# Feed-forward in a two-block transformer kernel: sixteen of 22 inner chunks as Strassen products of halves

## The chip, the core and the metric

One core of a Trainium2 chip runs the whole program. The metric is device time in microseconds (us) of one execution; lower is better. Three runs of the kernel before took 3705.26, 3708.18 and 3711.72 us, median 3708.18.

## The reference, cut to what matters

The program is two blocks of a network on 512 tokens of width 1024. The change touches only the feed-forward of the second block, which runs four times (`ffn1` and `ffn2` in each of two layers):

```python
D_MODEL, SEQ, DEPTH = 1024, 512, 2
D_FF = ((8 * D_MODEL // 3 + 127) // 128) * 128      # 2816 = 22 chunks of 128
def rmsnorm(x, g):
    xf = x.astype(jnp.float32)
    y = xf * lax.rsqrt(jnp.mean(xf * xf, axis=-1, keepdims=True) + NORM_EPS)
    return (y * g.astype(jnp.float32)).astype(x.dtype)
def swiglu(h, w_in, w_out):
    gate, up = jnp.split(h @ w_in, 2, axis=-1)
    return (jax.nn.silu(gate) * up) @ w_out
# per layer:
x = x + 0.5 * swiglu(rmsnorm(x, ffn1_norm[layer]), ffn1_w_in[layer], ffn1_w_out[layer])
...
x = x + 0.5 * swiglu(rmsnorm(x, ffn2_norm[layer]), ffn2_w_in[layer], ffn2_w_out[layer])
```

All of it is float32.

## The kernel before

Activations lie feature-major: `self.x` is eight tiles of 128 features by 512 tokens. A float32 product is made of three TensorE products in the format float32r: `split` (lines 112 to 115) writes a high part (a rounded copy, on ScalarE, L114) and a low part (the difference, on VectorE, L115), and `mm3` (L131 to L133) adds high·high, low·high and high·low in PSUM. `weight` loads 128x1024 weights (512 KB) by the SP queue (L121) into one of three staging buffers, and splits them into `wh` and `wl` (four buffers each). `fm` does one such load and its matmuls: for a chunk of 128 output features, 8 blocks of 128 inputs, so 8 x 3 = 24 matmuls with 128x128 stationary weights and 512 moving columns (the tokens).

`ffn` (L1185) goes over the 22 inner chunks in three groups of 8, 8 and 6. A chunk takes two `fm`, one for the gate and one for the up part, 48 matmuls. The normalisation's factor per token, `rb`, is not in the moving tiles: it is multiplied in afterwards, on VectorE into the gate (L1196), after the SiLU (L1197, ScalarE) once more on GpSimd (L1198); then VectorE multiplies by the up part (L1200) and the result is split. After a group, eight `fm` with the group's chunks as inputs add the group's share of the output to `self.x` (L1211, VectorE, factor 0.5). In the last feed-forward the last group is done in two halves of 256 tokens, each followed by the final norm.

PSUM tiles come from eight banks by name: `p3` has three, `pS` two, `p1`, `pT` and `po` one each. The order of instructions on each engine is laid out at build time by a planner that simulates the program; inside `manual_schedule(engines={PE})` TensorE's order is instead that of the program text. Every engine works through its own queue in order, also past an instruction that waits.

Of the kernel before, what the change touches and what calls it, by code (L numbers as in the profile page):

```python
# [3 lines left out]

# [16 lines left out]
T = S + L  # L21
# [39 lines left out]
class Net:  # L61
# [65 lines left out]
    def mm3(self, pt, items, first=True, last=True):  # L127

        mm, n = self.nc.tensor.matmul, len(items)
        for i, (sh, sl, mh, ml) in enumerate(items):  # L130
# [36 lines left out]
def drain(gen):  # L167

    for _ in gen:
        pass  # L170
# [197 lines left out]
class Block1:  # L368
# [744 lines left out]
class Block2:  # L1113
# [67 lines left out]
        self.net.nc.vector.tensor_tensor(self.x[c], ps, self.x[c], op=OP.add)  # L1181


    def ffn(self, n, l, cuts=((0, S),), after=None):

        net, nc = self.net, self.net.nc
        win, wout = net.I[f"{n}_w_in"], net.I[f"{n}_w_out"]
        drain(self.norm(f"{n}_norm_2", l))
        with net.tc.tile_pool(name=f"{n}{l}", bufs=3) as pool:
            for k0, kn in ((0, 8), (8, 8), (16, 6)):  # L1190
                hid = []
                for j in range(k0, k0 + kn):
                    pg = self.fm(win[l, j], self.h)
                    pu = self.fm(win[l, 22 + j], self.h)
                    t = pool.tile([P, S], F32, name="g", tag="g")
                    nc.vector.tensor_tensor(t, pg, self.rb, op=OP.mult)  # L1196
                    nc.scalar.activation(t, t, AF.Silu)  # L1197
                    nc.gpsimd.tensor_tensor(out=t, in0=t, in1=self.rb, op=OP.mult)  # L1198
                    u = pool.tile([P, S], F32, name="u", tag="u")
                    nc.vector.tensor_tensor(u, pu, t, op=OP.mult)  # L1200
                    hi = pool.tile([P, S], F32R, name="hh", tag="hh", bufs=11)
                    lo = pool.tile([P, S], F32R, name="hl", tag="hl", bufs=11)
                    net.split(u, hi, lo)
                    hid.append((hi, lo))
                for t0, t1 in cuts if k0 == 16 else ((0, S),):
                    part = [(hi[:, t0:t1], lo[:, t0:t1]) for hi, lo in hid]
                    for c in range(8):
                        ps = self.fm(wout[l, c, :, k0 * P:(k0 + kn) * P], part,
                                     net.psum("ps" if after else None)[:, :t1 - t0])
                        x = self.x[c][:, t0:t1]  # L1210
                        nc.vector.scalar_tensor_tensor(x, ps, 0.5, x, op0=OP.mult, op1=OP.add)  # L1211
                    if after and k0 == 16:
                        after(t0, t1)


    def softplus(self, x, n, pool):
# [736 lines left out]
def model(ctx, tc, I, out):  # L1953
    net = Net(ctx, tc, I)
    with ExitStack() as one:
        net.setup(one)
        st = Start(net)
# [12 lines left out]
    b2 = Block2(net, st, b1.xres, ctx)  # L1970
    for l in range(DEPTH):
# [2 lines left out]
        b2.cross(l)  # L1974
        if l == 0:
            b2.ffn("ffn2", l)
    with tc.tile_pool(name="fin", bufs=1) as pool:
        b2.ffn("ffn2", 1, ((0, 256), (256, 512)), b2.final(out, pool))


# [134 lines left out]
```

## Time and profile before

| | |
|---|---|
| median of three runs | 3708.18 us |
| the profiled execution's own time | 3708.82 us |
| its span, first to last instruction | 3707.0 us |
| TensorE (PE) busy in the span | 3613.7 us, 97% |
| VectorE (DVE), ScalarE (ACT), GpSimd (POOL) | 56%, 37%, 19% |
| mean granted TensorE clock | 0.993 of full speed |
| DMA | 364 MB, mean 98 GB/s |

Matmuls are pipelined: a record of one lasts longer than the distance from one start to the next, so the work of TensorE is read from distances between starts. Views of the trace are named in words: the page's parts, groups of instructions by line, the timeline, windows, and the instructions of one line.

### The profile page before, as it was taken

The numbers are of one execution on the slowest core, as the hardware profiler recorded it, in microseconds if no ns is written. First come the engines' busy times: TensorE is split into PE (matmuls) and PEld (weight loads), VectorE is DVE, ScalarE is ACT, GpSimd is POOL, SyncE is SP. The second block draws the span as 40 slices with busy tenths as digits, with TensorE's granted clock in tenths as the row PEclk, the third lists the DMA queues.
The fourth block names the chain that finished last, engine by engine and source line by source line (L and its number), as shares of the span: only waits on it lengthen the run. The fifth ranks groups of instructions, "written<-read, shape, count | busy, mean of one in ns | idle before, by whom it ended". The sixth has DMA issues, their size and how long they took to land.

```text
span 3707.0 us, 51470 instructions
## 1 busy us (share of the span) xinstructions
PE 3613.7 (97%) x19706; PEld 2992.2 (81%) x19706; DVE 2060.9 (56%) x4228; ACT 1375.7 (37%) x2407; POOL 715.0 (19%) x889
## 2 busy tenths in 40 slices
PE   8999999999999999999999999999999999999998
PEld 6887778888887778888778888888888887788887
DVE  6565773366566464334666433443347887664335
ACT  4334443234345332224654322322233333443223
POOL 1222330002233011102320100210013444101001
PEclk9999999999999999999999999999999999999999
DMA  8434113243322333333122333333333212323333
GB/s 277 121 118 136 57 50 123 63 149 90 88 69 65 139 105 97 97 94 105 57 91 64 108 97 97 97 97 97 97 98 114 57 57 74 115 77 91 103 97 103
DMA packets 135718, 364.35 MB, mean 98 GB/s; under 512 B 30000, under 2 KB 43184, under 8 KB 134960
## 3 DMA queue, kind: packets, MB, share of 16 engines
q1 hardware_dynamic: 135472, 361.06, 31.6%
q8 instruction: 155, 2.54, 0.3%
q14 instruction: 91, 0.75, 0.1%
HBM read 331.64 MB, written 19.66 MB: 95 GB/s over the span
## 4 chain that ended last, share of the span: by engine, by line
PE 88%; DVE 6%; ACT 2%; DMA 2%; issue 1%; POOL 1%; SPq 0%; DVEq 0%; ACTq 0%; POOLq 0%
PE p L131 15%; PE p L133 15%; PE p L132 15%; PE pS L131 7%; PE pS L132 7%; PE pS L133 6%; PE po L519 2%; PE pT L132 2%; PE pT L131 2%; PE pT L133 2%; PE po L132 2%; PE po L133 2%; PE po L131 2%; DVE wl L115 1%; PE pS L493 1%
## 5 line engine op out<-in xcount | busy, mean ns | idle before, releaser
L114 ACT ACTIVATE wh<-ws 128x1024 fp32r<-128x1024 f32 (+4 forms) x561 | 563.8, 1006 | 1424.2 <-PE p L132 677.4
L115 DVE TENSOR_TENSOR wl<-ws,wh 128x1024 fp32r<-128x1024 f32 (+4 forms) x561 | 662.2, 1181 | 259.7 <-ACT wh L114 257.6
L131 PE MATMUL p<-nh,wh 128*128 128x512 f32 x1084 | 429.0, 397 | 4.5 <-ACT nh L1131 2.0
L133 PE MATMUL p<-nh,wl 128*128 128x512 f32 x1084 | 424.6, 392 | 4.5 <-DVE wl L115 4.5
L132 PE MATMUL p<-nl,wh 128*128 128x512 f32 x1084 | 423.8, 391 | 1.9 <-DVE nl L115 1.9
L1198 POOL TENSOR_TENSOR g<-g,rb 128x512 f32<-128x512 f32 x88 | 149.7, 1703 | 1137.2 <-ACT g L1197 1137.2
L131 PE MATMUL pS<-nh,wh 128*128 128x512 f32 x620 | 254.1, 410 | 1.0 <-DVE xr L1181 1.0
L133 PEld LDWEIGHTS p<-nh,wl 128*128 128x128 f32 x1084 | 203.4, 188 | 50.2 <-DVE wl L115 6.0
L133 PE MATMUL pS<-nh,wl 128*128 128x512 f32 x620 | 242.5, 391 | 0.0
L132 PE MATMUL pS<-nl,wh 128*128 128x512 f32 x620 | 242.2, 391 | 0.0
L131 PEld LDWEIGHTS p<-nh,wh 128*128 128x128 f32 x1084 | 203.6, 188 | 46.7 <-ACT nh L1131 2.5
L132 PEld LDWEIGHTS p<-nl,wh 128*128 128x128 f32 x1084 | 203.4, 188 | 42.4 <-DVE nl L115 2.2
L1196 DVE TENSOR_TENSOR g<-p,rb 128x512 f32<-128x512 f32 x88 | 60.5, 691 | 227.7 <-PE p L133 217.5
L131 PE MATMUL p<-hxh,wh 128*128 128x512 f32 (+1 forms) x456 | 183.2, 402 | 0.8 <-DVE wT L502 0.8
L132 PE MATMUL p<-hl,wh 128*128 128x512 f32 (+1 forms) x488 | 179.8, 369 | 0.0
L133 PE MATMUL p<-hh,wl 128*128 128x512 f32 (+1 forms) x488 | 179.4, 368 | 0.0
L131 PE MATMUL p<-hh,wh 128*128 128x512 f32 (+1 forms) x488 | 179.3, 368 | 0.0
L133 PE MATMUL p<-hxh,wl 128*128 128x512 f32 (+1 forms) x456 | 169.9, 373 | 0.0
L132 PE MATMUL p<-hxl,wh 128*128 128x512 f32 (+1 forms) x456 | 169.8, 372 | 0.0
L1140 POOL TENSOR_TENSOR acc<-acc,sq 128x512 f32<-128x512 f32 x48 | 73.6, 1533 | 481.5 <-ACT sq L1139 479.5
L509 POOL TENSOR_SCALAR p<-p,rinv 128x768 f32<-128x768 f32 (+2 forms) x128 | 103.3, 807 | 253.8 <-DVE rinv L508 143.7
L1211 DVE SCALAR_TENSOR_TENSOR xr<-p,xr 128x512 f32<-128x512 f32 (+1 forms) x68 | 42.5, 627 | 169.6 <-PE p L133 169.5
(591 smaller groups left out, 8780.8 us busy)
## 6 DMA issues: line engine op xcount, KB each, us to landing
ws<-in_ffn_w_in_dram SPq DMA_DIRECT2D x176, 512.0 KB
ws<-in_ffn_w_out_dram SPq DMA_DIRECT2D x64, 512.0 KB
ws<-in_w_in_tok_dram SPq DMA_DIRECT2D x52, 512.0 KB
wh<-in_w_ada_dram SPq DMA_DIRECT2D x48, 512.0 KB
ws<-in_ffn_w_out_dram SPq DMA_DIRECT2D x40, 384.0 KB
ws<-in_w_out_dram SPq DMA_DIRECT2D x24, 512.0 KB
ws<-in_dn_qkv_dram SPq DMA_DIRECT2D x24, 512.0 KB
ws<-in_xa_wk_dram SPq DMA_DIRECT2D x16, 512.0 KB
```

Of the source, the lines that this page charges most:

```text
L114: self.last_hi = self.nc.scalar.activation(hi, src, AF.Copy)
L115: (eng or self.nc.vector).tensor_tensor(out=lo, in0=src, in1=hi.bitcast(F32), op=OP.subtract)
L131: mm(pt, sh, mh, start=first and i == 0, stop=False)
L132: mm(pt, sh, ml, start=False, stop=False)
L133: mm(pt, sl, mh, start=False, stop=last and i == n - 1)
L493: mm(ps, q, kA[:, k0:k1], start=True, stop=False)
L509: nc.gpsimd.tensor_scalar(p, p, r, 0.5, op0=OP.mult, op1=OP.mult)
L519: self.net.nc.tensor.matmul(ps[h:h + HD, :], v, w, start=i < 2, stop=i >= len(parts) - 2)
L1140: (nc.vector if c == 7 else nc.gpsimd).tensor_tensor(out=acc, in0=acc, in1=sq, op=OP.add)
L1196: nc.vector.tensor_tensor(t, pg, self.rb, op=OP.mult)
L1198: nc.gpsimd.tensor_tensor(out=t, in0=t, in1=self.rb, op=OP.mult)
L1211: nc.vector.scalar_tensor_tensor(x, ps, 0.5, x, op0=OP.mult, op1=OP.add)
```

## The change

Six chunks at the head of each feed-forward stay as they were (`plain`), apart from the second multiplication by `rb`, which moves to VectorE. The other sixteen, in two groups of eight, are done by seven products of half size (Strassen's method in Winograd's form): the inputs are halved in features (512 each) and tokens (256 each), the gate and up weights of a chunk in their input features. A product has 4 blocks x 3 = 12 matmuls of 256 columns, so a chunk has 84. Banks `a` (P1, P6, P5, P3), `d` (P7, P4) and `e` (P2) add up products, and partial sums are copied out of `a` on the way.

The activation sums S1 to S4 are made once per feed-forward by `halves`, while the output of the first six chunks is multiplied. The weight sums T3, T2 and T4 of a chunk grow in one buffer: a plain SP load, then three DMAs on the GpSimd queue that add to what is there. T1 is a subtraction on VectorE. The high parts of five of the seven weight operands are copies on GpSimd, the other two on ScalarE; the seven low parts are on VectorE. The products P3 and P4 of a chunk are put between those of the next chunk.

```diff
+    USES = dict(P1=("X11", "B11"), P2=("X12", "B21"), P3=("S4", "B22"), P4=("X22", "T4"), P5=("S1", "T1"),
+                P6=("S2", "T2"), P7=("S3", "T3"))
+    def halves(self, name, l, pool, hold):
...
+        for c in range(8):
+            v = xg[c // 2].rearrange("p (h c t) -> p h c t", h=2, c=2)[:, :, c % 2, :]
+            nc.vector.scalar_tensor_tensor(v, halved(self.x[c]), g[:, c:c + 1], halved(self.rb), op0=OP.mult, op1=OP.mult)
...
+        def part(p):
+            (a11, a21), (a12, a22) = ((x[:, :S], x[:, S:]) for x in (xg[p], xg[2 + p]))
+            put("X11", p, a11)
+            s3 = tmp("s3", "t")
+            nc.vector.tensor_tensor(s3, a11, a21, op=OP.subtract)
+            put("S3", p, s3)
+            yield
...
+    def sums(self, wu, pool):
+        T, T1 = (pool.tile([P, 512], F32, name=n, tag=n, bufs=b) for n, b in (("T", 3), ("T1", 2)))
+        nc.sync.dma_start(T, wu[:, :512])
+        nc.gpsimd.dma_start(T, wu[:, 512:], accum_op=OP.add)
+        return dict(T1=T1, T3=T, T2=T, T4=T)
+    def parts(self, wg, wu, pool):
+        G, B22 = (pool.tile([P, w], F32, name=n, tag=n, bufs=2) for n, w in (("wg", 1024), ("wu", 512)))
+        nc.sync.dma_start(G, wg)
+        nc.sync.dma_start(B22, wu[:, 512:])
+        return dict(B11=G[:, :512], B21=G[:, 512:], B22=B22)
+    def operands(self, B, W, *names):
+        h = net.whi.tile([P, 1024], F32R, name="wh", tag="wh")
+        l = net.wlo.tile([P, 1024], F32R, name="wl", tag="wl")
+        for i, n in enumerate(names):
+            sl = slice(i * 512, (i + 1) * 512)
+            if n == "T1":
+                nc.vector.tensor_tensor(B["T1"], B["T2"], B["B22"], op=OP.subtract)
+            if n in ("T1", "B22"):
+                nc.scalar.activation(h[:, sl], B[n], AF.Copy)
+            else:
+                nc.gpsimd.tensor_copy(h[:, sl], B[n])
+            nc.vector.tensor_tensor(l[:, sl], B[n], h[:, sl].bitcast(F32), op=OP.subtract)
...
+    def product(self, n, W, ps, first=True):
+        x, b = self.USES[n]
+        wh, wl = W[b]
+        self.net.mm3(ps, [(wh[:, k, :], wl[:, k, :], *self.X[x][k]) for k in range(4)], first=first, more=not first)
+    def gated(self, pool, hold, hid):
+        ps = dict(a=net.psum("p3")[:, :H], d=net.psum("pS")[:, :H], e=net.psum("po")[:, :H])
...
+        def copy(n):
+            st[n] = small(n)
+            nc.scalar.activation(st[n], ps["a"], AF.Copy)
+        def gate(sl, snap, bank):
+            v = t[:, sl]
+            nc.vector.tensor_tensor(v, ps[bank], st[snap], op=OP.add)
+            nc.scalar.activation(v, v, AF.Silu)
+        def up():
+            copy("sU")
+            st["u1"] = small("u1")
+            nc.vector.tensor_tensor(st["u1"], ps["d"], st["sU"], op=OP.add)
+        def last():
+            gate(hi, "sV", "d")
+            nc.vector.tensor_tensor(u[:, hi], st["u1"], t[:, hi], op=OP.mult)
+            net.split(u, hd[:, :S], hd[:, S:])
+        return ps, dict(P1=lambda: copy("s1"), P7=lambda: None, P6=lambda: copy("sV"), P2=lambda: gate(lo, "s1", "e"), P5=up,
+                        P3=lambda: nc.vector.tensor_tensor(u[:, lo], ps["a"], t[:, lo], op=OP.mult), P4=last)
...
+    def ffn(self, n, l, out=None):
...
+            def operands(j, *names):
+                B = raw[j]
+                self.operands(B, W.setdefault(j, {}), *names)
+                for n, after, src in (("T2", "T3", win[l, j][:, :512]), ("T4", "T1", win[l, j][:, 512:])):
+                    if after in names:
+                        nc.gpsimd.dma_start(B[n], src, accum_op=OP.add)
+            K0 = 6
...
+            for k0, kn in ((K0, 8), (K0 + 8, 8)):
...
+                    for j in range(k0, k0 + kn):
...
+                        parts(j + 1)
+                        sums(j + 2)
+                        mm(j, made, "P1")
+                        mm(j, made, "P7")
+                        if more:
+                            operands(j + 1, "B11", "T3")
+                        if cur:
+                            mm(j - 1, cur, "P3")
+                        mm(j, made, "P6")
+                        if cur:
+                            mm(j - 1, cur, "P4")
+                        operands(j, "B22", "T4")
+                        mm(j, made, "P2")
+                        if more:
+                            operands(j + 1, "T2", "B21")
+                        mm(j, made, "P5")
+                        if more:
+                            operands(j + 1, "T1")
+                        cur = made
+                    mm(j, cur, "P3")
+                    mm(j, cur, "P4")
...
+                    self.ffn_out(wout[l], hid, k0, kn, -0.5)
```

The last feed-forward still does its last group (now eight chunks, before six) in two halves of 256 tokens.

## Rows read from the trace of the kernel before

**Rows 1.** The page, part 1: busy time, share, instructions of each engine.

```profile
PE 3613.7 (97%) x19706; PEld 2992.2 (81%) x19706; DVE 2060.9 (56%) x4228; ACT 1375.7 (37%) x2407; POOL 715.0 (19%) x889
```

**Rows 2.** Windows: 100 us of feed-forward; 40 us of the start.

```profile
core 0: us, PE busy (x) PEld busy (x) DVE busy (x) ACT busy (x) POOL busy (x), PEclk, DMA share, GB/s
3480.00:3580.00 100.00, 100.00 (x443) 82.81 (x442) 39.25 (x44) 26.23 (x31) 12.52 (x7) 1.00 0.33 96
...
20.00:60.00 40.00, 37.86 (x252) 27.61 (x251) 27.02 (x77) 14.46 (x24) 0.00 (x0) 1.00 0.94 312
```

**Rows 3.** Groups by line: feed-forward work beside TensorE; idle before, by whom.

```profile
L115 DVE TENSOR_TENSOR wl<-ws,wh 128x1024 fp32r<-128x1024 f32 x472 | 590.9, 1253 | 244.5 <-ACT wh L114 242.7
...
L114 ACT ACTIVATE hh<-u 128x512 fp32r<-128x512 f32 x88 | 55.7, 633 | 4.1 <-DVE u L1200 3.0
...
L1198 POOL TENSOR_TENSOR g<-g,rb 128x512 f32<-128x512 f32 x88 | 149.7, 1703 | 1137.2 <-ACT g L1197 1137.2
```

**Rows 4.** Timeline, DVE: the gate's multiplication of two successive chunks.

```profile
1626.80 0.69 DVE L1196 TENSOR_TENSOR g<-p,rb 128x512 f32<-128x512 f32 x1 [3.34 <-PE p L133]
...
1637.67 0.69 DVE L1196 TENSOR_TENSOR g<-p,rb 128x512 f32<-128x512 f32 x1 [2.70 <-PE p L133]
```

**Rows 5.** Timeline, PE: 16 successive matmuls of 512 columns, first and last.

```profile
1496.04 0.39 PE L131 MATMUL po<-nh,wh 128*128 128x512 f32 x1
...
1499.44 0.39 PE L131 MATMUL po<-nh,wh 128*128 128x512 f32 x1
```

**Rows 6.** Timeline, PE: 16 successive matmuls of 256 columns in the last group.

```profile
3658.16 0.28 PE L131 MATMUL p<-hh,wh 128*128 128x256 f32 x1
...
3659.96 0.28 PE L131 MATMUL p<-hh,wh 128*128 128x256 f32 x1
```

**Rows 7.** Timeline, DVE and POOL, a norm: successive operations with two SBUF inputs.

```profile
3326.67 1.85 DVE L1132 SCALAR_TENSOR_TENSOR nl<-xr,cols,nh 128x512 fp32r<-128x512 f32 x1
3326.68 1.29 POOL L1140 TENSOR_TENSOR acc<-acc,sq 128x512 f32<-128x512 f32 x1 [1.01 <-ACT sq L1139]
...
3328.44 0.68 DVE L1181 TENSOR_TENSOR xr<-p,xr 128x512 f32<-128x512 f32 x1
...
3329.04 1.21 DVE L115 TENSOR_TENSOR wl<-ws,wh 128x1024 fp32r<-128x1024 f32 x1
...
3330.18 0.74 DVE L1132 SCALAR_TENSOR_TENSOR nl<-xr,cols,nh 128x512 fp32r<-128x512 f32 x1
```

**Rows 8.** Instructions of a line, POOL: duration in ns, min/median/max.

```profile
L1330 POOL CAST dqh<-zero x8: 603/611/1493, 1745.4 to 1821.3; 64x512 fp32r<-64x512 f32 x8
...
L509 POOL TENSOR_SCALAR p<-p,rinv x128: 634/904/1978, 165.1 to 1225.1; 128x768 f32<-128x768 f32 x64, 128x448 f32<-128x448 f32 x32, 128x512 f32<-128x512 f32 x32
...
L1643 POOL MEMSET W<- x16: 514/515/528, 2768.7 to 3112.5; 128x512 f32 x16
```

**Rows 9.** Groups by line: operations on 256 and 768 columns.

```profile
L115 DVE TENSOR_TENSOR wl<-ws,wh 128x768 fp32r<-128x768 f32 x48 | 45.9, 955 | 6.0 <-ACT wh L114 5.7
...
L502 DVE COPY wT<-p 128x256 f32<-128x256 f32 x48 | 20.2, 421 | 23.6 <-PE p L851 23.3
...
L525 ACT ACTIVATE vl<-po 64x256 f32<-64x256 f32 x80 | 30.5, 381 | 57.7 <-PE po L519 48.4 <-issue 8.3
```

**Rows 10.** Timeline: an SP load of 384 KB, and who waited for it.

```profile
3664.95 0.33 SPq L121 DMA_DIRECT2D ws<-in_ffn_w_out_dram  x1
...
3668.18 0.85 ACT L114 ACTIVATE wh<-ws 128x768 fp32r<-128x768 f32 x1 [1.85 <-DMA ws<-in_ffn_w_out_dram]
```

More of the change, by code (lines that the diff above doesn't have):

```diff
@@ L2 @@
 from contextlib import ExitStack
+from functools import partial
 from itertools import chain, islice
@@ L125, in weight, with mm3 @@
         return h.rearrange("p (k c) -> p k c", k=nk), l.rearrange("p (k c) -> p k c", k=nk)
-    def mm3(self, pt, items, first=True, last=True):
+    def mm3(self, pt, items, first=True, last=True, more=False):
         mm, n = self.nc.tensor.matmul, len(items)
+        if more:
+            mm = partial(mm, skip_group_check=True)
         for i, (sh, sl, mh, ml) in enumerate(items):
@@ new lines, in plain, with evacuate @@
+    def plain(self, win, js, pool, hold, hid, stats):
+        net, nc = self.net, self.net.nc
+        def evacuate(pg, pu):
+            t = pool.tile([P, S], F32, name="t", tag="t", bufs=2)
+            u = pool.tile([P, S], F32, name="u", tag="u", bufs=2)
+            nc.vector.tensor_tensor(t, pg, self.rb, op=OP.mult)
+            nc.scalar.activation(t, t, AF.Silu)
+            nc.vector.tensor_tensor(t, t, self.rb, op=OP.mult)
+            nc.vector.tensor_tensor(u, pu, t, op=OP.mult)
+            hd = hold.tile([P, 2 * S], F32R, name="hd", tag="hd", bufs=10)
+            net.split(u, hd[:, :S], hd[:, S:])
+            hid.append((hd[:, :S], hd[:, S:]))
+        first = []
+        for i, tag in enumerate(("p3", "p3", "p3", "pS")):
+            first.append(self.fm(win[22 * (i % 2) + js[i // 2]], self.h, net.psum(tag)))
+            if i > 1:
+                next(stats)
+        evacuate(*first[:2])
+        evacuate(*first[2:])
+        for j in js[2:]:
+            evacuate(self.fm(win[j], self.h), self.fm(win[22 + j], self.h))
@@ L1206, in ffn @@
                     part = [(hi[:, t0:t1], lo[:, t0:t1]) for hi, lo in hid]
                     for c in range(8):
[L1208 to L1209 removed]
+                        ps = self.fm(wout[l, c, :, k0 * P:(k0 + kn) * P], part, net.psum("ps")[:, :t1 - t0])
                         x = self.x[c][:, t0:t1]
[L1211 removed]
@@ L1212, in ffn, with ffn_out, part @@
-                    if after and k0 == 16:
-                        after(t0, t1)
+                        nc.vector.scalar_tensor_tensor(x, ps, -0.5, x, op0=OP.mult, op1=OP.add)
+                    final(t0, t1)
+    def ffn_out(self, wout, hid, k0, kn, sign, steps=iter(())):
+        net, nc = self.net, self.net.nc
+        early = []
+        def part(c, ks):
+            if len(early) <= c:
+                early.append((net.psum(None), net.weight(wout[c, :, k0 * P:(k0 + kn) * P], kn)))
+            ps, (wh, wl) = early[c]
+            net.mm3(ps, [(wh[:, k, :], wl[:, k, :], *hid[k]) for k in ks], first=0 in ks, last=kn - 1 in ks)
+            if kn - 1 in ks:
+                nc.vector.scalar_tensor_tensor(self.x[c], ps, sign, self.x[c], op0=OP.mult, op1=OP.add)
+        for c in range(2):
+            part(c, range(kn - 1))
+        for c in range(2):
+            part(c, (kn - 1,))
+            next(steps, None)
+        for c in range(2, 8):
+            part(c, range(kn))
+            next(steps, None)
@@ L1976, in model @@
             b2.ffn("ffn2", l)
-    with tc.tile_pool(name="fin", bufs=1) as pool:
-        b2.ffn("ffn2", 1, ((0, 256), (256, 512)), b2.final(out, pool))
+    b2.ffn("ffn2", 1, out)
 def _constants():
```

104 lines of the change are left out of this document (86 added, 18 removed).

## The prediction

> **What bounds the kernel now.** I first read the page's busy times [rows 1]: TensorE 97%, no other engine over 56%. Then the windows of a stretch of feed-forward [rows 2]: TensorE is busy all 100 us of 100 at granted clock 1.00 (the 2.4 GHz level), VectorE 39 us, ScalarE 26, GpSimd 12.5, the DMA engines a third of the time. Then the groups by line [rows 3]: the weight splits and the GpSimd multiplication sit idle before their work, waiting for something that comes with TensorE's pace; nothing there waits long for them. So the feed-forward is TensorE's, and its price is the distance between matmul starts. With 512 columns 15 distances take 3.40 us, 0.2267 us each [rows 5]; with 256 columns, same 128x128 stationary tile, 15 take 1.80 us, 0.120 us each [rows 6]. That is 0.0133 us a matmul beside 0.4167 ns a column: half the columns cost 53% of the time, not 50%. A chunk before is 48 x 0.2267 = 10.88 us, and two successive chunks do stand 10.87 us apart [rows 4].
>
> **What is removed on the path.** A Strassen chunk is 84 x 0.120 = 10.08 us. The saving is 0.80 us a chunk; 16 chunks in 4 feed-forwards make 64, so **-51.2 us**. That is 7% of these chunks where the count of multiplications alone (7/8) would say 12.5%: the fixed part of a matmul is paid 84 times.
>
> **What is added on the path.**
> - The last feed-forward's last group has eight chunks where it had six, in halves of 256 tokens: two chunks x 8 outputs x 3 = 48 matmuls become 96 of half size, 48 x (0.240 - 0.2267) = **+0.6**.
> - At a group's end P3 follows P5 in the same bank and must wait for the copy of the partial sum. Nothing lies between them there. From the start of P5's last matmul: 0.28 until its record ends [rows 6], 0.38 for a ScalarE copy of 256 columns [rows 9], some 0.1 of signals, less the 0.12 that would pass anyway: 0.64. P4's wait (u1, 0.42 on VectorE) fits under P3's 1.44. Eight group ends: **+5.1**. Within a group two products lie between P5 and P3, so there this costs nothing.
> - The entry. While TensorE multiplies out the first six chunks (8 x 6 x 3 x 0.2267 = 32.6 us), VectorE makes the activation sums and low parts. Its pace is 0.60 us for 512 columns and 1.14 for 1024, start to start [rows 7]. 22 operations of `halves` 13.2, eight weight splits of 768 columns at about 0.87 (0.955 [rows 9] less the 0.08 by which starts overlap) 7.0, eight additions into x 4.8, the first chunk's operands 8 x 0.60 = 4.8, locks with five GpSimd copies 3 (below), the last plain chunk 1.8: 34.6, two more than its cover. Some (X12, S1, S4, X22) is needed only 4 to 10 us later. Between 0 and 4.8 (should the eight normalisations of `halves` fall here too) I take 1.5, nearer to the first since they can run from the time `rb` is known: x 4 = **+6.0**.
>
> **What is added beside the path.** Per chunk of 10.08 us:
> - ScalarE: casts of T1, B22 and the result at 0.63 [rows 3], three copies of 256 at 0.38 [rows 9], two half SiLUs at some 0.4: 3.8 us; 3.4 before. Hidden by slack of 6 us; without it the group-end stall would come in every chunk.
> - VectorE: seven low parts, T1 and the result's low part are 9 x 0.60; the half-width evacuations and the last product 5 x 0.33 (0.42 long [rows 9], less 0.09 overlap): 7.05 us; 4.1 before. Cover is TensorE's chunk, 3 us of it left.
> - GpSimd: five copies f32 to float32r of 512 columns. The same operation on 64 partitions took 0.61 us [rows 8]: 3.05 us. The multiplication by `rb` (1.7 us [rows 3]) goes.
> - Three accumulating DMAs on GpSimd's queue, each of 256 KB. No row has one. The issue costs GpSimd between 0.33 us (an SP issue [rows 10]) and 1.7 (its own two-input pass [rows 3]). A memset of 512 columns, which like an issue reads no tensor, took 0.51 [rows 8]; with a read and a write side to describe I take 1.0. SP's third load a chunk costs another 0.33 of an idle queue.
> - DMA engines: 1.05 MB plain and 0.79 MB accumulated a chunk. At 312 GB/s (94% busy) [rows 2] that is 5.9 us if an accumulated byte costs one plain byte, 8.4 if two, 10.9 if three; 2.7 fills TensorE's 10.08. I take two, as it reads two operands. The Trainium skill's "Collectives: The Full Stack", section "The bandwidth ceiling", says the same of the DMA engines' add: it is slower only because of its two source reads. No run here has shown that yet.
>
> **GpSimd and VectorE exclude each other.** A VectorE operation with two SBUF inputs, 0.74 us alone, lasted 1.85 when it started beside a GpSimd addition of 1.29 [rows 7]: it waited it out. A single-input GpSimd operation, too, ranges from 0.63 to 1.98 us on line 509 [rows 8]. With nine such VectorE operations and five GpSimd copies a chunk, 5.4 + 3.05 = 8.45 us must share that way; if all copies fall into VectorE's working time, its chunk is 7.05 + 3.05 = 10.1 us, exactly TensorE's. "SBUF — State Buffer" of the Trainium skill, section "Who interferes with whom", makes it a full lock for every GpSimd operation that reads SBUF, copies included, which fits the row; were copies exempt, VectorE would keep 3 us of slack, and the +12.8 below would be 0.
>
> **What is late next: the loop through GpSimd's queue.** T3, T2, T4 share a buffer, so each accumulation waits for the readers before it, and the next copy waits for the accumulation. The queue is in order: behind a copy of T2 that waits for its DMA stand T4's accumulation, the next chunk's copies of B11 and T3, and behind those the next T2. Round trip: T2 copy 0.61, its low part and T1 1.2, issue of T4 1.0, B11 and T3 copies 1.22, T3's low part 0.6, sum 4.6; then the accumulation, issue 1.0 and landing. A plain 384 KB load was 3.2 us from issue to use [rows 10]; I take this for landing, twice that as the upper end, and less cannot be counted on for 256 KB of read-and-add. That is 8.8 us; if VectorE's evacuations and the other copies' low parts all fall in between (2.8), 11.6. The middle is 10.2, TensorE's pace. I take 0.2 us late a chunk, between 0 and 1.5: 64 x 0.2 = **+12.8**. Loads of G and B22 come a chunk ahead and cost nothing as long as landing stays under some 10 us.
>
> **Sum.** -51.2 + 0.6 + 5.1 + 6.0 + 12.8 = -26.7 us. The profiled execution took 3708.8 (span 3707.0 and 1.8 around it), 0.6 above the median of the runs; from the median, **3681.5 us**.
>
> **The rivals.**
> - *Fed freely.* The planner keeps all operands ahead, no entry stall: -51.2 + 0.6 + 5.1, so 3663. For: 3 us slack on VectorE and GpSimd each. Against: the lock. Chance 0.08.
> - *The lock binds.* VectorE's 10.1 us with its waits for ScalarE and GpSimd in an in-order queue becomes the chunk, 10.65 us: 64 x (10.65 - 10.88) + 11.7 (the other three terms) = -3, 3705. For: the wait of 1.1 us on record [rows 7]. Against: the evacuations from PSUM can run beside copies. Chance 0.12, two thirds of it within the bound of no change.
> - *The accumulations bind: slower.* Place: the copy of T2 in GpSimd's queue. If landing is twice the plain load's (6.5 us), the loop is 4.6 + 1.0 + 6.5 = 12.1 us a chunk: 64 x 1.22 + 11.7 = +90, 3798. It decides from a loop of 10.7, an accumulation of 6.1 us from issue to landing; a DMA cost of three plain bytes does the same. For: nothing in the trace bounds it, and the loop has no slack at the price that I took. Against: plain transfers fill only a third of the DMA engines now [rows 2]. Chance 0.22.
> - *The arithmetic is not cheaper.* If weight loads, one for each matmul, could not keep up with 256 columns, 84 small matmuls would cost as much as 48 large from 0.130 us a start on. Rows 6 show 0.120 in a long stretch with the same stationary size, so this has no chance of its own.
>
> **The numbers.** About 0.2% (7.4 us) is what a measurement of this kernel can tell from no change. The forecast (0.58) has its own range of 3657 to 3700. Faster: 0.58 + 0.08 + 0.03 = 0.69; same 0.08; slower 0.22 + 0.01 = 0.23. The range takes in the forecast, the free feed down to 3657, the lock, and the milder half of the accumulations' case, to 3745 (a loop of 11.3 us).
>
> **What would show it.** Right: 256-column matmuls 0.120 us apart in long runs; chunks 10.1 to 10.4 us apart (successive SiLUs of one half); TensorE idle some 0.6 us before the P3 at group ends; GpSimd 60 to 75% busy in these stretches, VectorE 70% or more, DMA share 0.6 to 0.85. Wrong: TensorE idle in each chunk before the first matmul of P6 or P4, released by VectorE's low part after a GpSimd copy that waited for a DMA (the loop); low parts of 1 us and more with GpSimd copies beside them in every chunk (the lock); the granted clock falling to the 1.2 GHz level in gaps, which would price them double; or an idle TensorE at the seventh chunk of over 2 us (the entry).

## The result, and the profile after

The changed kernel takes 3866.8 us (median of four runs, 3861.82 to 3871.92) where the kernel before took 3707.44 in the runs beside it: a ratio of 1.043, 95% interval 1.0415 to 1.0446. It is slower by 159 us; the prediction was 3681.5, with a range of 3657 to 3745.

The page of the changed kernel, parts 1, 3, 5 and 6. The columns of part 3 are packets, MB and share of the 16 DMA engines; part 5 gives busy us, mean ns of one, idle before and its releaser.

```profile
span 3870.2 us, 58287 instructions
...
PE 3650.2 (94%) x22058; PEld 3124.4 (81%) x22058; DVE 2443.4 (63%) x4948; ACT 1423.4 (37%) x2719; POOL 998.9 (26%) x1313
...
q1 hardware_dynamic: 144688, 362.12, 30.0%
q0 software_dynamic: 27648, 50.34, 8.4%
...
L1270 POOL CAST wh<-T 128x512 fp32r<-128x512 f32 x192 | 176.7, 920 | 216.7 <-DMA T<-in_ffn_w_in_dram 196.5
...
L1360 POOL DMA_DIRECT2D T<-in_ffn_w_in_dram x128 | 119.8, 936 | 147.4 <-DVE wl L1271 142.3
...
T<-in_ffn_w_in_dram POOLq DMA_DIRECT2D x192, 256.0 KB, 4.5
```

TensorE fell from 97% to 94% of a longer span [rows 1], so it waits now. GpSimd's casts of the weight sums stood idle 196.5 us for the accumulating DMAs; the accumulating issues of L1360 stood idle 142.3 us for VectorE's low parts. An accumulation takes 4.5 us from issue to landing.

Windows of the changed kernel (columns as in [rows 2]): a group of eight Strassen chunks, and a stretch outside.

```profile
1459.00:1560.00 101.00, 85.25 (x638) 82.69 (x636) 68.13 (x102) 28.82 (x64) 46.53 (x55) 0.93 0.64 134
1712.00:1760.00 48.00, 48.00 (x214) 39.75 (x213) 26.14 (x42) 19.91 (x29) 11.31 (x10) 1.00 0.35 103
```

In the group TensorE is idle 16 us of 101 and its granted clock is 0.93; outside it is busy throughout at 1.00, as before the change [rows 2]. The chunk's length is the distance between the copies of one partial sum, `sV`. The first and the eighth of this group, in ScalarE's timeline:

```profile
1462.12 0.38 ACT L1293 ACTIVATE sV<-p 128x256 f32<-128x256 f32 x1 [0.87 <-PE p L136]
...
1556.62 0.36 ACT L1293 ACTIVATE sV<-p 128x256 f32<-128x256 f32 x1
```

Seven distances in 94.5 us, 13.5 each; the eight groups give 13.1 to 14.1, mean 13.52, where a chunk was 10.88 and 10.08 was due. This settles where the time is: 56 distances x (13.52 - 10.88) = +148. From the last `sV` of a first group to the first of the second, one chunk's work and the second layer, 56.8 us pass on average where 10.88 + 192 x 0.2267 = 54.4 did: 4 x 2.4 = +10. That is 158 of the 163 us by which the span of this profiled execution, 3870.2, is longer than the 3707.0 before.

One turn of a chunk in the timeline of the changed kernel (start, duration, engine, line, operation, idle before):

```profile
1490.07 0.42 DVE L1297 TENSOR_TENSOR t<-pS,sV 128x256 f32<-128x256 f32 x1 [3.29 <-PE pS L136]
...
1490.41 0.68 DVE L1271 TENSOR_TENSOR wl<-T,wh 128x512 fp32r<-128x512 f32 x1
...
1491.39 0.86 POOL L1360 DMA_DIRECT2D T<-in_ffn_w_in_dram  x1 [3.15 <-DVE wl L1271]
...
1496.19 0.69 DVE L1266 TENSOR_TENSOR T<-T,wu 128x512 f32<-128x512 f32 x1 [0.76 <-DMA T<-in_ffn_w_in_dram]
1496.22 1.14 POOL L1270 CAST wh<-T 128x512 fp32r<-128x512 f32 x1 [2.80 <-DMA T<-in_ffn_w_in_dram]
...
1496.80 1.10 DVE L1271 TENSOR_TENSOR wl<-wg,wh 128x512 fp32r<-128x512 f32 x1
...
1497.63 0.28 PE L135 MATMUL p<-nh,wh 128*128 128x256 f32 x1
...
1498.15 2.38 DVE L1271 TENSOR_TENSOR wl<-T,wh 128x512 fp32r<-128x512 f32 x3
...
1499.98 0.58 PE L136 MATMUL p<-nh,wl 128*128 128x256 f32 x1 [2.07 <-DVE wl L1271]
...
1500.22 0.86 POOL L1360 DMA_DIRECT2D T<-in_ffn_w_in_dram  x1 [0.84 <-DVE wl L1271]
...
1500.36 0.42 PE L134 MATMUL p<-nh,wh 128*128 128x256 f32 x1
...
1500.58 0.42 PE L135 MATMUL p<-nh,wh 128*128 128x256 f32 x1
...
1501.05 0.68 DVE L1271 TENSOR_TENSOR wl<-T,wh 128x512 fp32r<-128x512 f32 x1
...
1502.80 0.86 POOL L1246 DMA_DIRECT2D T<-in_ffn_w_in_dram  x1 [1.71 <-DMA T<-in_ffn_w_in_dram]
...
1503.34 1.22 POOL L1360 DMA_DIRECT2D T<-in_ffn_w_in_dram  x1
```

Read it downwards. VectorE waits 3.29 us for TensorE's P4 of the chunk before, and only then makes the low part of T3. That lets GpSimd issue T2's accumulation (1491.39). 4.83 us later it has landed and the cast of T2 starts (1496.22). VectorE makes T1's subtraction (L1266) and B21's low part first, the latter 1.10 us long beside GpSimd's cast, and then three low parts of T's; TensorE waits 2.07 us for one of these in P6. T4's accumulation goes out at 1500.22. The next chunk's low part of T3 is done at 1501.73, but its T2 accumulation stands in GpSimd's queue behind the issue of a later T3 (L1246), which waits 1.71 us for its plain load, and goes out at 1503.34: 11.95 us from T2 to T2. And the gap costs more than itself: the matmuls after it start 0.21 to 0.22 us apart, not 0.12, until 1503.3. The window of these microseconds, of the same kernel:

```profile
1500.40:1503.20 2.80, 2.80 (x15) 2.80 (x15) 1.33 (x3) 0.00 (x0) 1.09 (x2) 0.50 0.84 190
```

The granted clock is 0.50, the 1.2 GHz level, after an idle of 2.07 us, with TensorE busy all the while. TensorE's waits by line say the same of the whole run (total us, times, longest):

```profile
PE p L136 <- DVE wl L1271: 91.1, 53, 2.4
PE p L134 <- POOL wh L1270: 22.6, 26, 2.5
PE p L134 <- ACT sU L1293: 13.1, 7, 4.1
```

The first of these is the sign that the prediction named for the loop: TensorE idle before a low part that VectorE makes late.

### The profile page after: what moved, and what is told of

It reads as the page before. It is cut to its first block, busy times and chain, and to the rows that moved or that the text cites. A ratio compares the mean times of both kernels' runs of the same rounds, so it can differ in the third digit from the quotient of the medians.

```text
span 3870.2 us, 58287 instructions
## 1 busy us (share of the span) xinstructions
PE 3650.2 (94%) x22058; PEld 3124.4 (81%) x22058; DVE 2443.4 (63%) x4948; ACT 1423.4 (37%) x2719; POOL 998.9 (26%) x1313
## 3 DMA queue, kind: packets, MB, share of 16 engines
q1 hardware_dynamic: 144688, 362.12, 30.0%
q0 software_dynamic: 27648, 50.34, 8.4%
## 5 line engine op out<-in xcount | busy, mean ns | idle before, releaser
L115 ACT ACTIVATE wh<-ws 128x1024 fp32r<-128x1024 f32 (+3 forms) x433 | 428.4, 993 | 861.0 <-PE p L135 297.5
L116 DVE TENSOR_TENSOR wl<-ws,wh 128x1024 fp32r<-128x1024 f32 (+3 forms) x433 | 505.9, 1172 | 243.6 <-ACT wh L115 242.1
L136 PE MATMUL p<-nh,wl 128*128 128x256 f32 (+1 forms) x1244 | 432.6, 348 | 94.7 <-DVE wl L1271 91.1
L134 PE MATMUL p<-nh,wh 128*128 128x256 f32 (+1 forms) x1244 | 434.2, 349 | 40.3 <-POOL wh L1270 22.6
L135 PE MATMUL p<-nl,wh 128*128 128x512 f32 (+1 forms) x604 | 239.4, 396 | 4.0 <-DVE nl L1135 2.2
L134 PE MATMUL pS<-nh,wh 128*128 128x512 f32 (+1 forms) x620 | 236.4, 381 | 1.9 <-DVE xr L1184 1.0
L1270 POOL CAST wh<-T 128x512 fp32r<-128x512 f32 x192 | 176.7, 920 | 216.7 <-DMA T<-in_ffn_w_in_dram 196.5
L136 PE MATMUL pS<-nh,wl 128*128 128x512 f32 (+1 forms) x620 | 223.0, 360 | 0.0
L1271 DVE TENSOR_TENSOR wl<-T,wh 128x512 fp32r<-128x512 f32 x256 | 199.3, 804 | 4.8 <-POOL wh L1270 3.7
L135 PE MATMUL p<-nh,wh 128*128 128x256 f32 x640 | 183.5, 287 | 0.0
L135 PE MATMUL p<-hd,wh 128*128 128x512 f32 (+1 forms) x448 | 161.2, 360 | 2.5 <-DVE hd L116 2.5
L134 PE MATMUL p<-hd,wh 128*128 128x512 f32 (+1 forms) x448 | 160.5, 360 | 0.8 <-ACT wh L115 0.8
L1360 POOL DMA_DIRECT2D T<-in_ffn_w_in_dram x128 | 119.8, 936 | 147.4 <-DVE wl L1271 142.3
```

Source lines behind the costliest of these rows:

```text
L115: self.last_hi = self.nc.scalar.activation(hi, src, AF.Copy)
L116: (eng or self.nc.vector).tensor_tensor(out=lo, in0=src, in1=hi.bitcast(F32), op=OP.subtract)
L1270: nc.gpsimd.tensor_copy(h[:, sl], B[n])
L1271: nc.vector.tensor_tensor(l[:, sl], B[n], h[:, sl].bitcast(F32), op=OP.subtract)
L1360: nc.gpsimd.dma_start(B[n], src, accum_op=OP.add)
```

## The experiments

Each edit is made to the changed kernel. A chunk's length is the mean distance of successive copies of `sV`, as above; where "most" chunks or a chunk "inside a group" are named, it is the distance that recurs there. The medians of the kernel before lay between 3705.2 and 3708.1 us beside all these runs.

**Buffers.** One more buffer for the weight sums.

```diff
-for n, b in (("T", 3), ("T1", 2))
+for n, b in (("T", 4), ("T1", 2))
```

> Edit: the buffer T in which a chunk's weight sums grow has four places instead of three, nothing else. In the changed kernel the accumulation of the next-but-one chunk stands in GpSimd's queue ahead of T2's and waits for a plain load that can start only when a place is free (72 us of such waits in the run, 1.1 us a chunk). Theory A, the loop of accumulations through GpSimd's in-order queue: that wait leaves the loop, 3790 to 3830 us, chunks 12.4 to 12.9 us apart instead of 13.5. Theory B, the lock between GpSimd's copies and VectorE's subtractions sets the pace: nothing is taken from it, within 10 us of the changed kernel's 3867.

Measured: 3858.5 us, ratio 1.0405 (1.0389 to 1.0420), a chunk about 13.4: within theory B's 10 us. But theory A's premise was hardly met: GpSimd still waits 60 us for those plain loads (72 before), and its casts wait 178 us for the DMAs (197 before). So this run does not decide between them; the next ones do.

**No accumulating DMAs.** They are left out, so that the weight sums are incomplete.

```diff
-        nc.gpsimd.dma_start(T, wu[:, 512:], accum_op=OP.add)
...
-                        nc.gpsimd.dma_start(B[n], src, accum_op=OP.add)
```

> Edit: the three accumulating DMAs a chunk are left out, and with them their part of the weight sums (T3, T2 and T4 are then the plain loaded half of the up weights); all copies, subtractions and products stay, GpSimd's copies too. Theory A (loop): chunks 10.1 to 10.5 us apart, 3665 to 3695 us. Theory B (lock): 13 us and more, 3840 us or over, since 8.5 us of exclusive work and VectorE's waits stay.

Measured: 3689.8 us, ratio 0.9959 (0.9945 to 0.9974). The window of a group in this run:

```profile
1459.00:1540.00 81.00, 81.00 (x662) 80.26 (x661) 63.03 (x105) 26.90 (x61) 26.89 (x36) 1.00 0.33 105
```

TensorE is busy 81 us of 81 at granted clock 1.00, and a chunk takes 10.21 us, 10.1 inside a group. So the cheaper arithmetic is there, and all of the loss hangs on the three DMAs. The casts on GpSimd, still there, cost nothing inside a group.

**The high parts on ScalarE, the DMAs kept.**

```diff
-            if n in ("T1", "B22"):
-                nc.scalar.activation(h[:, sl], B[n], AF.Copy)
-            else:
-                nc.gpsimd.tensor_copy(h[:, sl], B[n])
+            nc.scalar.activation(h[:, sl], B[n], AF.Copy)
```

> Edit: all seven high parts on ScalarE, none on GpSimd; the three accumulating DMAs stay. ScalarE then has 3.8 + 5 x 0.63 = 7.0 us a chunk. Theory B (lock): the whole loss goes, chunks 10.1 to 10.4 us apart, 3665 to 3690 us. Theory A (loop): three copies of 0.9 us leave the loop and GpSimd no longer holds them behind an accumulation, but 0.9 us of issue and 4.5 us of landing twice a chunk stay: chunks 11 to 12 us apart, 3715 to 3780 us.

Measured: 3791.2 us, ratio 1.0224 (1.0207 to 1.0241), a chunk about 12.1: a little over theory A's ranges and far from B's. The waits of this run:

```profile
DVE T L1266 <- DMA T<-in_ffn_w_in_dram: 206.7, 61, 5.4
ACT wh L1267 <- DMA T<-in_ffn_w_in_dram: 169.8, 94, 5.6
```

The wait for the DMA moved with the casts into ScalarE's queue, and stayed in VectorE's, where T1's subtraction waits for T2. Freeing GpSimd's queue of the casts takes 1.4 us off the chunk's excess of 3.4.

**The sums on VectorE.** T3, T2 and T4 by additions from SBUF; first with all casts on ScalarE.

```diff
+                if "T3" in names:
+                    nc.vector.tensor_tensor(B["T3"], B["T3"], B["B22"], op=OP.add)
-                        nc.gpsimd.dma_start(B[n], src, accum_op=OP.add)
+                        nc.vector.tensor_tensor(B[n], B[n], B[src], op=OP.add)
```

> Edit: the three weight sums are additions on VectorE (3 x 0.60 us) from the plain loaded parts, no accumulating DMA; all high parts on ScalarE. VectorE then has 8.85 us a chunk, ScalarE 7.0, GpSimd nothing. Theories A and B both expect the loss gone, chunks 10.1 to 10.5 us apart, 3665 to 3695 us. A third, C, that the products themselves (order, banks, copies out of the accumulating bank, 256 columns) cost more than 84 x 0.120 us whatever feeds them, expects over 3740.

Measured: 3700.3 us, ratio 0.9978 (0.9969 to 0.9987), a chunk 10.3 inside a group: the loss is gone, 5 us above the expected range. Then the same additions with the five casts left on GpSimd:

> Edit: as e4 the three sums are additions on VectorE, but five high parts stay on GpSimd. Against e4 this is the price of the lock alone, with VectorE at 8.85 us a chunk of which 7.5 has two SBUF inputs, and GpSimd's copies at 3.05. Rival C (the lock): 8.85 + 3.05 = 11.9 us a chunk at most, 11 to 12 us apart, 3735 to 3800 us. If the copies fit beside the work from PSUM, 10.3 to 10.5 us, within 10 us of e4's 3700.

Measured: 3695.1 us, ratio 0.9964 (0.9951 to 0.9978). The window of a group in this second run:

```profile
1459.00:1540.00 81.00, 80.06 (x652) 78.59 (x650) 77.32 (x129) 28.71 (x62) 32.47 (x36) 1.00 0.33 105
```

GpSimd's casts of the sums in the same run (ns, min/median/max):

```profile
L1269 POOL CAST wh<-T x192: 612/1067/1073, 1449.2 to 3620.1; 128x512 fp32r<-128x512 f32 x192
```

Here VectorE is busy 77 us of 81, and the median cast of a sum takes 1.07 us, where it took 0.62 in the run without the DMAs and without these additions; the chunk is 10.3 all the same, as with the casts on ScalarE. The Trainium skill's "SBUF — State Buffer", section "Who interferes with whom", has a VectorE instruction with two SBUF inputs contend with any GpSimd instruction that reads SBUF; these casts agree. But TensorE waits for none of them in this run.

**One sum by DMA, off the loop.** As the first of these two, but T3 by its accumulating DMA, two chunks ahead of its use.

> Edit: as e4 (high parts on ScalarE, T2 and T4 by additions on VectorE), but T3 again by the accumulating DMA, which is issued two chunks ahead and waits for no reader. VectorE then has 8.25 us a chunk. Theory A (the loop: it is the accumulation's way through waits and queues between two uses that costs): chunks 10.1 to 10.3 us apart, 3680 to 3695 us, a little under e4. Rival B (an accumulating DMA costs wherever it stands, by its load on the DMA engines or its issue): over 3705.

Measured: 3694.5 us, ratio 0.9960 (0.9948 to 0.9973), a chunk 10.3 inside a group, with landings of 3.9/5.0/8.3 us (min/median/max). A third of the accumulated bytes, as slow as before to land, and no harm: for this sum it is the place in the chain that counts, not the DMA. All three off the loop were not tried.

**Plain loads in place of the accumulating ones.**

```diff
-nc.gpsimd.dma_start(T, wu[:, 512:], accum_op=OP.add)
+nc.gpsimd.dma_start(T, wu[:, 512:])
```

and likewise for T2 and T4.

> Edit: the changed kernel with the three DMAs of a chunk on GpSimd's queue as plain loads in place of accumulating ones, at the same places, with the same waits before and behind them; the additions of the weight sums are left out by this. Theory A (loop of issue, landing and in-order queues): most of the loss stays, as a plain load lands only some 1 us earlier: chunks 11.5 to 13 us apart, 3760 to 3840 us. Rival B (the adding in the DMA engines, 178 ns a packet instead of 84): chunks 10.1 to 10.6, 3675 to 3710 us.

Measured: 3783.2 us, ratio 1.0206 (1.0190 to 1.0221), a chunk about 11.9. Landing is 2.7/3.2/7.2 us against 3.8/4.5/8.8, GpSimd's issue 0.54 us long against 0.86. A cheaper transfer gives back half of the loss (84 of 159 us), not more.

**Own buffers.** As the last, but T3, T2 and T4 each in buffers of their own, so that a load no longer waits for the readers of another sum. T4 and T1 have one place each, so T4's load still waits for the readers of the chunk before, and T3 has two places where T had three.

> Edit: as e6 (three plain loads on GpSimd's queue, the additions left out), but T3, T2 and T4 have buffers of their own (two, two and one place, T1 one), so that a load does not wait for the readers of the sum before it; same DMAs, same places in the queue, same copies on GpSimd. Theory A: the chain is cut, chunks 10.1 to 10.6 us apart, 3675 to 3715 us. If it stays within 30 us of e6, it is the number of DMAs on GpSimd's queue or their issue time beside the copies that costs, not the chain.

Measured: 3760.5 us, ratio 1.0142 (1.0126 to 1.0157): not the 3675 to 3715 of the theory, and, at 23 us from the last run, within the 30 for which the expectation names the DMAs' number and issue time. Most chunks take 10.1 to 10.9 us, but in each group two to four take 11.6 to 15.2. Issues on GpSimd still wait 91 us in all for VectorE's low parts, with casts behind them, and 68 us for plain loads. In the first of the long chunks (15.18 us) VectorE waits 2.60 us for TensorE's P3 at 1492.44 with low parts of sums queued behind it, and TensorE then waits 1.5 and 2.0 us for low parts. So part of this is again the order of the queues; the parts were not told apart.

**A later issue of the next sum.** The accumulation for T3 goes behind T4's cast, since GpSimd waited 72 us at the head of a chunk for the plain load before it.

```diff
+            def add(j):
+                if j < 22:
+                    nc.gpsimd.dma_start(raw[j]["T3"], win[l, 22 + j][:, 512:], accum_op=OP.add)
...
                         operands(j, "B22", "T4")
+                        add(j + 2)
```

> The changed kernel with one issue moved: the accumulating DMA of a chunk's sum T3 is put into GpSimd's queue half a chunk later, behind the cast of T4, so that it no longer stands ahead of the casts while the plain load of its own tile is under way; all the work and all DMAs stay. Theory A (in-order queues around the loop cost as much as the landing itself): the 72 us in which GpSimd waited for that plain load go, and part of them comes off the chunk: 12.4 to 13.2 us a chunk, 3800 to 3850 in all. Theory B (the chain of DMA, cast, low part, DMA alone sets the pace): the chunk stays within 0.2 us of 13.5 and the time within 15 us of the changed kernel's 3867.

Measured: 3868.0 us, ratio 1.0440 (1.0423 to 1.0457), a chunk about 13.4: the numbers of theory B. But the wait did not go: GpSimd still waits 74 us, 37 times, for the plain loads at this issue (72 us, 39 times, before), since its order is the planner's and not that of the program text. So what that wait costs is not shown here.

**Program order for VectorE and GpSimd.** The wait of 3.29 us at 1490.07 suggested that the order of the queues closes the loop.

```diff
-                with net.tc.manual_schedule(engines={mybir.EngineType.PE}):
+                with net.tc.manual_schedule(engines={mybir.EngineType.PE, mybir.EngineType.DVE, mybir.EngineType.Pool}):
```

> The changed kernel, with VectorE and GpSimd as well as TensorE held to program order in the Strassen chunks; every DMA, cast and addition stays. In the order that the planner gave them, VectorE's low part of a chunk's T3 stands behind the gate's addition of the chunk before, which waits for TensorE's P4 (the wait at 1490.07, 3.29 us), and GpSimd's accumulating issue for T2 waits for that low part with the cast of T4 queued behind it, which TensorE's next P4 needs: the loop goes once round TensorE, VectorE, GpSimd and a DMA for each chunk. In program order the low part of T3 comes first. Theory A (the order of the two queues, not the landing, closes the loop): a chunk at 10.1 to 10.6 us, the whole at 3680 to 3715. Theory B (a chain of issue, landing of 4.5 us, cast, low part, twice a chunk, is too long in any order): a chunk stays over 12.5 us, the whole over 3800.

Measured: 3951.6 us, ratio 1.0661 (1.0645 to 1.0678): theory A falls. But the chunks came out regular, most 12.4 to 12.7 us (mean 12.97, with 14 to 18 at the head of a group). One turn, GpSimd's and VectorE's timeline of this run:

```profile
1506.09 0.86 POOL L1360 DMA_DIRECT2D T<-in_ffn_w_in_dram  x1 [1.45 <-DMA T<-in_ffn_w_in_dram]
...
1510.25 0.67 POOL L1270 CAST wh<-T 128x512 fp32r<-128x512 f32 x1 [2.69 <-DMA T<-in_ffn_w_in_dram]
...
1510.96 1.07 DVE L1271 TENSOR_TENSOR wl<-T,wh 128x512 fp32r<-128x512 f32 x1 [0.17 <-POOL wh L1270]
1511.95 0.68 DVE L1271 TENSOR_TENSOR wl<-wg,wh 128x512 fp32r<-128x512 f32 x1
1512.55 0.41 DVE L1304 TENSOR_TENSOR u<-pS,sU 128x256 f32<-128x256 f32 x1
1512.88 0.68 DVE L1266 TENSOR_TENSOR T<-T,wu 128x512 f32<-128x512 f32 x1
1514.10 0.86 POOL L1360 DMA_DIRECT2D T<-in_ffn_w_in_dram  x1 [2.62 <-DVE T L1266]
...
1514.64 1.21 POOL L1246 DMA_DIRECT2D T<-in_ffn_w_in_dram  x1
1515.18 1.29 POOL L1270 CAST wh<-wg 128x512 fp32r<-128x512 f32 x1
1515.73 1.29 POOL L1270 CAST wh<-T 128x512 fp32r<-128x512 f32 x1
1516.50 1.07 DVE L1271 TENSOR_TENSOR wl<-wg,wh 128x512 fp32r<-128x512 f32 x1 [1.50 <-POOL wh L1270]
1517.50 0.68 DVE L1271 TENSOR_TENSOR wl<-T,wh 128x512 fp32r<-128x512 f32 x1
```

T2's issue to its cast 4.16; its cast to T4's issue 3.85 (two low parts, an evacuation, T1, and 0.54 from T1's end at 1513.56 to the issue); T4's issue to the cast of B11 1.08 (two issues); that cast to the next T2's issue, 1518.47, 3.29 (two casts, two low parts; the low part of T3 ends at 1518.18 and lets it go): 12.38 us. The next turn starts where this one ends. So there is a loop once a chunk with one landing in it, and order alone does not open it.

**Only VectorE in program order; the next sum later; ScalarE too.** Three variants of that run, in this order:

> As the run before, but VectorE alone is held to program order beside TensorE; GpSimd's queue is left to the planner. If VectorE's order closes the loop alone: within 15 us of the run with both. If GpSimd's order (an accumulating issue ahead of a cast that TensorE needs sooner) takes part: 3730 to 3830.

> As the run with VectorE and GpSimd in program order, and the accumulating DMA of T3 issued half a chunk later, behind the cast of T4, so that GpSimd doesn't wait for the plain load at the head of a chunk. Theory A (order closes the loop): within 10 us of the run with both queues in program order, and faster by up to 10 if the wait at the chunk's head still delays the casts. Theory B (the landings are too long in any order): over 3800.

> As the run with VectorE and GpSimd in program order, with ScalarE in program order too. Theory A: within 15 us of that run, since ScalarE was idle two thirds of the time; in program order its cast of T1 stands behind the copy of P5 and ahead of the silu of the next gate, so a loss of up to 1 us a chunk, 64 us, is possible if the cast of T1 then waits for the DMA of T2 with a copy out of a bank queued behind it. Theory B: over 3800.

Measured: 4028.7 (ratio 1.0875, 1.0852 to 1.0898), 3922.6 (1.0586, 1.0566 to 1.0606) and 3988.7 us (1.0759, 1.0738 to 1.0780). None opened the loop. VectorE in program order against a GpSimd in the planner's was the worst, a chunk 14.2, outside both of its expectations. With the next sum's issue behind the cast of T4, 0.54 in place of 1.08 us pass from T4's issue to the cast of B11; most chunks were 12.1, 0.3 less, and the whole 29 us less. ScalarE in program order cost 37 us, within the loss that was thought possible.

**Program order in the chunks alone.** In the run with both queues in program order, 70.4 us passed between two groups: VectorE's weight splits of the second layer stood behind additions that wait for TensorE.

```diff
                     mm(j, cur, "P4")
+                with net.tc.manual_schedule(engines={mybir.EngineType.PE}):
```

> As the run with VectorE and GpSimd in program order, but in the Strassen chunks alone; the second layer behind each group is left to the planner on these two engines. There VectorE's low parts of the weights stood behind additions into x that wait for TensorE, and the way from one group to the next took 70.4 us in place of some 55. If that explains why the run was slower than the changed kernel although its chunks were shorter (12.4 to 13.0 against 13.5): 3805 to 3845, with chunks still at 12.4. If the loss lies elsewhere: over 3900.

Measured: 3822.8 us, ratio 1.0312 (1.0295 to 1.0329), as expected, with most chunks at 12.4 again. Against the changed kernel it gains 44 us of the 159 by the order of the two queues alone. Of the 115 that remain, 86 are 56 distances of 12.42 in place of 10.88: the loop.

**The same with plain loads**, to see the landing alone.

> As the run before with plain loads in place of the accumulating ones, so that the weight sums are incomplete: T3, T2 and T4 hold the block that was loaded last. Landing fell from 4.5 us to 3.2 in the first run with plain loads. Theory A (a loop once a chunk in the queues: issue of T2's DMA to its cast 4.16, cast of T2 to issue of T4's DMA 3.85, two issues 1.08, cast of B11 to the next issue of T2's 3.29, together 12.4): only the first term shrinks, by 1.3, and a chunk takes 11.0 to 11.3 us. Theory B (bandwidth or traffic of the accumulating DMAs sets the pace): the pace falls to TensorE's 10.1 to 10.4. Theory C (landing doesn't matter): 12.4 as before.

Measured: 3764.8 us, ratio 1.0156 (1.0141 to 1.0171), chunks mostly 11.4. One turn in GpSimd's timeline of this run:

```profile
1508.72 0.54 POOL L1360 DMA_DIRECT2D T<-in_ffn_w_in_dram  x1 [1.45 <-DVE wl L1271]
...
1511.68 1.11 POOL L1270 CAST wh<-T 128x512 fp32r<-128x512 f32 x1 [1.81 <-DMA T<-in_ffn_w_in_dram]
...
1516.44 0.54 POOL L1360 DMA_DIRECT2D T<-in_ffn_w_in_dram  x1 [2.63 <-DVE T L1266]
...
1517.50 0.62 POOL L1270 CAST wh<-wg 128x512 fp32r<-128x512 f32 x1
...
1520.13 0.54 POOL L1360 DMA_DIRECT2D T<-in_ffn_w_in_dram  x1 [1.45 <-DVE wl L1271]
```

The same four terms are 2.96, 4.76, 1.06 and 2.63, together 11.41. So the chunk is 1.0 less for 1.2 less from T2's issue to its cast, near theory A's 11.0 to 11.3 and far from TensorE's 10.1; but two of the other terms moved too, by +0.91 and -0.66, which theory A had not: T2's low part now stands behind more of VectorE's queue. The traffic is not the pace; the loop is.

**The entry.** The kernel with one sum by DMA, and the one with VectorE's sums and GpSimd's casts, with the plain chunks left to the planner's order on TensorE as before the change.

```diff
-            with net.tc.manual_schedule(engines={mybir.EngineType.PE}):
-                hid = []
-                self.plain(win[l], range(K0), pool, hold, hid, stats)
+            drain(stats)
+            hid = []
+            self.plain(win[l], range(K0), pool, hold, hid, stats)
+            with net.tc.manual_schedule(engines={mybir.EngineType.PE}):
```

> As the run with T3 by one accumulating DMA, T2 and T4 by additions on VectorE and the casts on ScalarE, with one thing put back as it was before the change: the six plain chunks at the head of each feed-forward, and the norm's statistics ahead of them, are left to the planner's order on TensorE and not to program order. Theory A (program order of TensorE at the norm costs some 3 us in gaps and in columns at the lower clock, in each of four feed-forwards): 3680 to 3688. Theory B (the entry's loss is the extra work of the halves on VectorE, which stays): within 4 us of 3694.5.

> As the run with all three sums by VectorE additions and five high parts cast on GpSimd, with the six plain chunks at the head of each feed-forward left to the planner's order on TensorE. Theory A (program order at the norm costs some 3 us in each feed-forward): 3681 to 3689, within 6 us of the run with one accumulating DMA and planned start. Theory B (the halves on VectorE cost it): within 4 us of 3695.

Measured: 3692.3 (ratio 0.9958, 0.9943 to 0.9973) and 3687.2 us (0.9945, 0.9929 to 0.9962). The first says theory B, the second A. The second's profiled execution is 4.7 us shorter than that of the same kernel with the start in program order (7.8 in the medians), and all of that is there by the first group (its first `sV` at 1459.3 against 1464.2 us); the other three entries add nothing. The cost of program order at the norm stays open. The last is the fastest kernel here, 20 us (0.55%) under the one before.

## Why the prediction was wrong

**What held.** 256-column matmuls stand 0.12 us apart where TensorE is fed, and a chunk without the DMAs takes 10.1 us inside a group: the -51.2 was real (10.21 with a group's edges, 56 distances x -0.67 = -38 measurable between copies). The accumulated byte costs two plain ones: 8.4% of the DMA engines for 50.34 MB is 0.167% per MB, 30.0% for 362.12 MB is 0.083, a factor of 2.0; as plain loads the same 50.34 MB took 4.2%. The Trainium skill's "Collectives: The Full Stack", section "The bandwidth ceiling", puts the slowness of a ReduceScatter, whose DMAs add, down to the add's two source reads; the factor measured here agrees. Issue and landing were taken as 1.0 + 3.2 = 4.2 and measured 4.5 (4.16 and 4.83 in the turns shown). The lock of GpSimd and VectorE was read rightly and does not bind by itself (3689.8 and 3695.1 with the casts on GpSimd), so that rival is out. Nor would the +12.8 have been 0 without it, as the prediction has it: with no cast on GpSimd and the DMAs kept (3791.2), 84 us of loss remain.

**The step that failed: the loop's "sum 4.6", and the middle taken above it.** The loop was named with its right members, and its landing was sized rightly. What lies between landings was not. The prediction counted the copy of T2, its low part and T1 as 1.8; it took 3.85, because VectorE's queue holds B21's low part and an evacuation between them, the first low part of each pair lasts 1.07 in place of 0.68 beside the cast of the other half, and 0.54 pass before the issue. It counted the copies of B11 and T3 and T3's low part as 1.8; it took 3.29, with casts at 1.29 behind two issues and B11's low part ahead of T3's. The issues, 1.0, took 1.08. So 8.2 stands where 4.6 did, and 8.2 + 4.16 is 12.4 us where the middle, 10.2, was taken. The prediction had evacuations and other low parts at 2.8 if all fell in between, and took half of that; even so its upper end, 11.6, was too low. An in-order queue has to be walked with all that stands in it; a sum of the links of the dependence chain is its lower bound, and "the middle" had no row behind it. 0.2 us late a chunk became 3.4 (13.52 against 10.08), 2.3 of them by the loop of 12.4; with the other terms as forecast, the +12.8 would have had to be +199.

**The rest of the loss.** The order that the planner gave VectorE and GpSimd adds some 44 us more (3866.8 against 3822.8). In it the low part of T3 sometimes waits for TensorE's P4, as in the turn shown, and chunks of 14 to 17 us stand beside ones of 11 or 12; that the one makes the other is not shown chunk by chunk. The falling clock was named as what would price gaps double, and it did add to them: in the eight groups' windows it was 0.89 to 0.93. How the excess of 3.4 us a chunk divides between idle time and clock can be read in the group shown (16 us of 101 idle, so 2.1 us of 13.5, and 1.3 at the lower clock); whether the loop would be shorter at full clock was not tried.

**The rival that came true came for another reason.** *The accumulations bind* had the place, the side and the sign, but its condition, an accumulation of 6.1 us or three plain bytes, was not met. At 4.5 us it should not have bound. The loop of 10.7 from which it was to decide was passed by the other terms. A chance of 0.22 was therefore too low: it was hung on the wrong unknown.

**Smaller terms.** Group ends were taken as 0.64 us each, +5.1, on the ground that nothing lies between P5 and the copy that P3 waits for. At seven of the eight ends TensorE waited 1.36 to 1.67 us there in the run with VectorE's sums and GpSimd's casts (10.5 us in all), and 1.36 to 3.63 in the run without the DMAs. One end in the first of these:

```profile
1539.05 1.06 ACT L115 ACTIVATE wh<-ws 128x1024 fp32r<-128x1024 f32 x1 [0.48 <-PE p L135]
...
1540.01 0.37 ACT L1292 ACTIVATE sU<-p 128x256 f32<-128x256 f32 x1
...
1540.43 0.39 PE L134 MATMUL p<-nh,wh 128*128 128x256 f32 x1 [1.36 <-ACT sU L1292]
```

The copy stands in ScalarE's queue behind a cast of the second layer's weights: a small case of the same step, a chain counted without the queue that it goes through. The entries, +6.0, come out as a small difference of large numbers: with VectorE's sums, -13.1 measured, less 56 x -0.46 = -26.0 and 4 x 0.8 = +3.3 between the groups, leaves +10; the planned start leaves +2. The +6.0 lies between; no more can be said. *Fed freely* (3663) was met by no run: with TensorE busy throughout inside a group, the run without the DMAs still stands 27 us above it, at the edges of groups and in the entries.

## What to carry to other kernels

When work in one buffer goes reader, DMA, reader, write down every instruction of each in-order queue between one issue and the next, in the order in which it stands there, and add up durations as they are beside their neighbours; compare that with the pace of the engine to be fed before asking what a DMA costs. Here one accumulating DMA was harmless two chunks ahead of its use (3694.5 us), three inside such a loop were ruinous (3866.8), and three additions on VectorE, which had room, were the better price (3695.1, and 3687.2 with the planned start). When a gap opens on TensorE, read the granted clock behind it as well: here the stretch after one gap of 2.07 us ran at the 1.2 GHz level. And before a run is taken as proof that a wait costs nothing, see whether the wait is gone in its trace.

## What the runs showed of the hardware

- The accumulating issue on GpSimd lasts 0.86 us in the records against 0.54 for a plain one, yet casts behind it start 0.54 us after it; a cast that starts so lasts 0.93 to 1.3 us, where 0.61 is one alone. The cast of 1.29 us at 1515.18 had no VectorE operation beside it. So part of the issue's time seems to be found in the instruction after it.
- 256 KB by GpSimd's queue landed 3.2 us after the issue in the median when plain, 4.5 when accumulating, 5.0 and 5.6 in two of the runs.
- After an idle of 2.07 us on TensorE (and 0.19 shortly before it) the next 3 us ran at a granted clock of 0.50, while the group of the run with VectorE's sums and GpSimd's casts, idle 0.94 us of 81 in all, shows 1.00.
